# Placing the side work of a layer kernel by estimated engine clocks

## Chip, cores and metric

One core of a Trainium2 chip runs the whole kernel in one launch. The metric is the device time in microseconds, from the first to the last instruction and what lies around it. TensorE is called PE, VectorE DVE, ScalarE ACT, GpSimd POOL and SyncE, which issues nearly all DMAs, SP.

## What is computed

One layer of an encoder over 1280 tokens (1024 of one request, 256 of another), ten tiles of 128 tokens, model width 2048:

```python
hn = rms_norm(x, norm_g)
proj = hn @ w_in                       # 2048 x 4896
xbc, z_ssd, dt_raw, q, k, v, z_att, mq, z_mem = split_cols(proj, IN_SIZES)
xbc = silu(centred_dwconv(xbc, conv_w, conv_b))
y = y_f + y_b + d_skip[:, None] * xs   # chunked state-space scan, forward and backward
o_ssd = rms_norm(y * silu(z_ssd))      # in two groups
o_att = window_attention(q, k, v, sink) * silu(z_att)    # 8 heads, 2 key heads, window 128
o_mem = softmax(mq @ mk.T) @ mv * silu(z_mem)            # 4 heads, 256 memory rows
return x + concat([o_ssd, o_att, o_mem]) @ w_out
# in a chunk of the scan, per head:
decay = exp(where(tril, acs[:, None] - acs[None, :], -inf))
y_diag = ((C @ B.T) * decay) @ (x * dt)
```

## The kernel before

All large products are done in fp32 accuracy with split operands: each operand is a high part in a one-pass format and a low part, and a product is three matmuls (L258, L259, L260; in the paired form L1158, L1159, L1160). ACT makes the high part of a weight row (`wh`, L208), DVE the low part (`wl`, L209). The ten token tiles are two groups of five. The rows of the current group's input stand split in SBUF as `xH` and `xL`, sixteen places of 128 rows each.

Order of the program: memory keys and values; `q` of group 1; paired blocks for the gates and the convolution channels of group 1; `kv` of group 1; `q` of group 0; paired blocks of group 0; then from about 757 us blocks of group 0 (`kv`, `mq`, `z0`, `z1`), of group 1 (`z0`, `z1`, `mq`), and the output projection: four blocks of group 0, and the paired blocks of group 1.

A block (`block_tok`) loops over sixteen weight rows k and five token tiles t, and yields after t = 1, after t = 3 and at the end of a row. At each yield `pump` advances side work, the lanes. A lane is a queue of Python generators; `step` runs one to its next `yield` and so puts its instructions into the program there. Lane 0 holds what attention needs: `mk_prep`, `k_prep`, `attn`, `mem_attn`. Lane 1 holds `dt_prep`, `ssd_one` and `ssd_two`, the scan. Each lane gets a fixed allowance per weight row (`RATES`, some 4 steps), and the number of bare `yield` lines between two parts of a generator sets the time that DMAs and engines have in between. `need` steps a lane until a named piece is done; the refill of the input places with output rows calls it, and a place in the third output block runs all lanes out.

A compile-time scheduler then orders the instructions of each engine; lane instructions of ACT and DVE are held behind the last weight split by `issue_after(marks)`. Each engine works its queue in order, so an instruction that waits holds those behind it.

Pieces that the change touches:
- `attn` loads and normalises the queries of a tile, splits and transposes them (`qh`, `pq`), then for four pairs of heads `scores` (`psc`, two key heads in one step), softmax in the same step, `turn_` (transposes `ppt`, L620), `values` (`po`).
- `mem_attn` the same with memory rows (`pmq`, `pms`, `pmt`, `pmo`).
- `ssd_one` does states and the decay matrix of a tile together. `rows` (L796) loads two broadcast tiles, `rf` and `rb`; `expo` (L866) adds a per-partition bias to each of four column blocks of both; `choose` (L871, L872) merges them and takes one exponential; `weights` (L876) multiplies; `diag` (`py`, L883) is the product.
- `p_fill` (L1189 to L1192) first normalises and splits the input rows of a group. The refill beside group 0's last `z1` block does so again for group 1: load `chd` (L192), scale with `rbc` (L196), split (L199, L200). `x_rows` (`prx`, L1368) makes `rbc`, three times in all.
- Tiles: `wa` five buffers, `wb` four, `rf` two, `rb` three, `ya` two; three PSUM banks `mix` for all lane work.

Of the kernel before, what the change touches and what calls it, by code (L numbers as in the profile page):

```python
# [28 lines left out]
CH, WB, RB, WA, WBB = 4, 3, 4, 5, 4  # L29
RBB = 3  # L30

RATES = {'kv': (2.0, 1.5), 'mq0': (3.9, 4.2), 'z0': (3.9, 4.2), 'z1': (3.9, 4.2), 'mq1': (3.9, 4.2), 'o': (3.5, 3.7)}
# [5 lines left out]
R_G, R_MG, R_SG, R_CB, R_CW, R_N = 0, 16, 32, 40, 52, 112  # L38


@with_exitstack
def hymba_encoder_kernel(
# [7 lines left out]
    V, A, G, T, S = nc.vector, nc.scalar, nc.gpsimd, nc.tensor, nc.sync  # L50
# [21 lines left out]
    dr = ctx.enter_context(tc.tile_pool(name="dr", bufs=1, space=bass.MemoryType.DRAM))  # L72

# [42 lines left out]
    sb_d = [dram([P, 1024], f"sb_{t}") for t in range(NT)]  # L116
    mk_d = dram([P, 4, 256], "mk_d")
# [19 lines left out]
    lanes = (deque(), deque())  # L137
    turn = [0]

    done = set()  # L140
# [7 lines left out]
    def step(lane):  # L148
        name, gen = lane[0]
        try:  # L150

            with ExitStack() as st:
                for ins in marks:
                    st.enter_context(tc.issue_after(ins))
                next(gen)
        except StopIteration:
            lane.popleft()
            done.add(name)

    owed = [0.0, 0.0]  # L160

    def pump(rates):

        for i in range(2):
            owed[i] = owed[i] + rates[i] if lanes[i] else 0.0
        while max(owed) >= 1:
            i = turn[0] ^ 1
            i = turn[0] = i if owed[i] >= 1 else i ^ 1
            owed[i] -= 1
            if lanes[i]:  # L170
                step(lanes[i])

    def need(fn, ts):

        for t in ts:
            while (fn.__name__, t) not in done:
                step(next(x for x in lanes if any(nm == (fn.__name__, t) for nm, _ in x)))


# [56 lines left out]
    def block_tok(w, nt, evac, before_last=None, feats=range(KT), places=range(KT)):  # L236
# [4 lines left out]
        for k in range(KT):  # L241
# [12 lines left out]
            for t in range(nt):  # L254
# [9 lines left out]
                if nt == 5 and t in (1, 3):  # L264
                    yield 0.8 if k == KT - 1 else 0.4
# [91 lines left out]

    def ev_mk(i, ps):
# [9 lines left out]
    def mk_prep(i):  # L368
        kr = w2("mkr")
# [4 lines left out]
        sq = w2("sq")  # L374
        rm = rx[:, 10 + i:11 + i]
        A.activation(sq, kr, AF.Square, scale=rm)
        V.reduce_sum(out=ss, in_=hv(sq, 4), axis=AX.X)
        r = sm.tile([P, 4], F32, tag="s4", name="r", bufs=4)
        rsqrt(r, ss, 1.0 / P, 4)
        yield  # L380
        yield
        V.scalar_tensor_tensor(out=hv(kr, 4), in0=hv(kr, 4), scalar=rm, in1=hb(r, 4, P), op0=ALU.mult, op1=ALU.mult)
        V.tensor_mul(hv(kr, 4), hv(kr, 4), gm.unsqueeze(1).broadcast_to([P, 4, P]))
        yield
        yield
# [4 lines left out]
        if i < 2:  # L390
            A.activation(mkH[:, :, c], hv(ps, 4), AF.Copy)
            V.tensor_sub(mkL[:, :, c], hv(ps, 4), mkH[:, :, c].bitcast(F32))
        else:
            o = w2("mko")
            A.activation(o, ps, AF.Copy)
            S.dma_start(mk_d[:, :, c], hv(o, 4))
        yield

    def mem_values(b):

        S.dma_start(mv, mv_d[:, 2 * b:2 * b + 2, :])
        yield
        yield
# [5 lines left out]
    def mem_swap(_):  # L409

        for b in range(2):
            k = w2("mki")
            S.dma_start(hv(k, 2), mk_d[:, 2 * b:2 * b + 2, :])
            hh = mkH[:, 2 * b:2 * b + 2, :]
# [5 lines left out]
    def k_prep(t):  # L420
        r = w2("kr")[:, :P]
# [3 lines left out]
        yield  # L425
        ss = sm.tile([P, 2], F32, tag="s2", name="kss", bufs=4)
        sq = w2("ksq")[:, :P]
        A.activation(sq, r, AF.Square)
        V.reduce_sum(out=ss, in_=hv(sq, 2), axis=AX.X)
        rr = sm.tile([P, 2], F32, tag="s2", name="krr", bufs=4)  # L430
        rsqrt(rr, ss, 1.0 / 64, 2)
        yield
# [3 lines left out]

        kh = mp.tile([P, 4, 2, 64], F32R, tag="wa", name="kh", bufs=WA)
        for d in range(2):
            A.activation(kh[:, 0:2, d, :], r3, AF.Copy)
        for d in range(2):  # L440
            V.tensor_sub(kh[:, 2:4, d, :], r3, kh[:, 0:2, 0, :].bitcast(F32))
        yield
        yield
        yield
# [8 lines left out]
        yield  # L453

    def kv_shift(_):

        V.tensor_copy(kT[:, :, 0:2 * P], kT[:, :, 3 * P:5 * P].bitcast(F32))
        V.tensor_copy(kL[:, :, 0:2 * P], kL[:, :, 3 * P:5 * P].bitcast(F32))
        V.tensor_copy(v_all[:, 0:2, :], v_all[:, 3:5, :])
        yield  # L460

    def slot(t):
        return t if t < 5 else t - 3

    def dt_prep(t0):
        for t in range(t0, t0 + 5):
            S.dma_start(dt_all[:, t, :], kv_d[t][:, :32])
        yield
        yield
        yield  # L470
# [3 lines left out]
        wj, dd = [a[:, slot(t0):slot(t0) + 5, :].rearrange("p t h -> p (t h)") for a in (wj_all, dd_all)]  # L474
        t5 = lambda a: a.rearrange("p (t h) -> p t h", t=5)
        x = flat(dt_all)
        V.tensor_add(t5(x), t5(x), dtb.unsqueeze(1).broadcast_to([P, 5, 32]))
        e, s = [mp.tile([P, 512], F32, tag="xs", name=n, bufs=2)[:, :160] for n in "es"]
        w, l = [mp.tile([P, 512], F32, tag="ya", name=n, bufs=2)[:, :160] for n in "wl"]
        V.scalar_tensor_tensor(out=e, in0=x, scalar=-1.0, in1=x, op0=ALU.mult, op1=ALU.min)  # L480
        A.activation(e, e, AF.Exp)
        V.tensor_scalar(out=s, in0=e, scalar1=2.0, scalar2=None, op0=ALU.add)
# [3 lines left out]
        V.tensor_scalar(out=e, in0=w, scalar1=1.0 / 17, scalar2=None, op0=ALU.mult)  # L486
        for c in (15, 13, 11, 9, 7, 5, 3):
# [4 lines left out]
        yield  # L492

        da = e
        V.tensor_mul(t5(da), dt_all[:, ts, :], aneg.unsqueeze(1).broadcast_to([P, 5, 32]))
        yield

# [3 lines left out]
        yield  # L501
        yield
        lower = w2("lower")[:, :P]
        G.affine_select(out=lower, in_=ones, compare_op=ALU.is_ge, fill=0.0, base=0,
                        pattern=[[-1, P]], channel_multiplier=1)
        yield
# [5 lines left out]
        ac = wb("ac", shape=(P, 512))  # L512
        A.activation(ac[:, :320], ps[:, :320], AF.Copy)
        for _ in range(2):
            A.activation(s, l, AF.Exp)
            d = da
# [4 lines left out]
            V.scalar_tensor_tensor(out=l, in0=d, scalar=2.0, in1=l, op0=ALU.mult, op1=ALU.add)  # L521
        A.activation(flat(eacs_all), ac[:, 0:160], AF.Exp)
        A.activation(flat(cd_all), ac[:, 160:320], AF.Exp)
        V.tensor_sub(wj, l, ac[:, 0:160])
        V.tensor_add(dd, wj, ac[:, 160:320])
        A.activation(dd, dd, AF.Exp)
        yield
# [3 lines left out]
        acT = wb("acT", shape=(P, 512))  # L531
# [4 lines left out]
        yield  # L536


    def attn(t):
# [8 lines left out]
        q = w2("q")  # L548
        S.dma_start(q, q_d[t])
        yield  # L550
        sq = w2("sq")
        A.activation(sq, q, AF.Square)
        ss = sm.tile([P, 8], F32, tag="s8", name="qss", bufs=4)
        V.reduce_sum(out=ss, in_=hv(sq), axis=AX.X)
        r = sm.tile([P, 8], F32, tag="s8", name="qr", bufs=4)
        rsqrt(r, ss, 1.0 / 64, 8)
        G.tensor_tensor(out=r, in0=r, in1=pow8, op=ALU.mult)
        for _ in range(3):
            yield
        q3 = hv(q)  # L560
        V.tensor_mul(q3, q3, hb(r, 8, 64))
        yield
        qT, parts = [], []
        for b in range(2):
            qh = mp.tile([P, 4, 2, 64], F32R, tag="wa", name="qh", bufs=WA)
            qb = q3[:, 4 * b:4 * b + 4, :]
            A.activation(qh[:, :, 0, :], qb, AF.Copy)
            V.tensor_sub(qh[:, :, 1, :], qb, qh[:, :, 0, :].bitcast(F32))
            parts.append(qh)
            yield  # L570
        yield
        for b, qh in enumerate(parts):
            ps = psum("pq")
            qf = qh.rearrange("p a b d -> p (a b d)")
            for a in range(4):
                T.transpose(ps[:, a * P:(a + 1) * P].bitcast(F32R), qf[:, a * P:(a + 1) * P], identr)
            o = mp.tile([P, 512], F32R, tag="qT", name="qT", bufs=2)
            A.activation(o, ps, AF.Copy)
            qT.append(o)
            yield  # L580
        z = w2("za")
        S.dma_start(hv(z, 4), zT_d[0][grp][:, :, tc_])
        yield
# [3 lines left out]
        def scores(rr):  # L587
            lg = mp.tile([P, 2, 384], F32, tag="lg", name="lg", bufs=2)
            nm = sm.tile([P, 2], F32, tag="m2", name="nm", bufs=10)
            for kv in range(2):  # L590
                h = 4 * kv + rr
                ps = psum("psc")
                st = qT[kv][:, rr * P:(rr + 1) * P]
                T.matmul(ps[:, :nk], st, kT[:, kv, s0 * P:s0 * P + nk], start=True, stop=False)
                T.matmul(ps[:, :nk], st, kL[:, kv, s0 * P:s0 * P + nk], start=False, stop=True)
                V.tensor_tensor_reduce(out=lg[:, kv, :nk], in0=ps[:, :nk], in1=ndist[:, d0:d0 + nk],
                                       scale=-2.0 ** -(h + 1), scalar=nsink[:, h:h + 1], op0=ALU.add, op1=ALU.min,
                                       accum_out=nm[:, kv:kv + 1])
            es = sm.tile([P, 2], F32, tag="m2", name="es", bufs=10)
            G.tensor_tensor(out=es, in0=sk8[:, rr, :], in1=nm, op=ALU.add)  # L600
            den = sm.tile([P, 2], F32, tag="m2", name="den", bufs=10)
# [3 lines left out]
            A.activation(es, es, AF.Exp)  # L605
            V.tensor_add(den, den, es)
            V.reciprocal(out=den, in_=den)
            for kv in range(2):
# [3 lines left out]
        def turn_(rr):  # L612
            lg = state_.pop(rr)
            if rr % 2 == 0:
                state_["pT"] = mp.tile([P, 2, 2, 384], F32, tag="pT", name="pT", bufs=1)
            pT = state_["pT"]
            for kv in range(2):
# [332 lines left out]
    def ssd_two(t):  # L950
# [49 lines left out]
        if first:  # L1000
# [5 lines left out]
            for g in range(2):  # L1006
                turn_ssd(g)
                yield

# [632 lines left out]
```

## Time and profile before

| | |
|---|---|
| median of three runs | 1817.0 us (1814.24 to 1818.96) |
| the profiled execution | 1821.53 us |
| its span, first to last instruction | 1819.8 us |
| mean granted PE clock | 0.994 |
| PE busy | 1777.1 us, 98% |
| ACT, DVE, POOL busy | 1003.1, 1331.6, 676.9 us |
| DMA | 297.49 MB, mean 163 GB/s |

Busy time of PE counts from start to the modelled end of each matmul, and these overlap; a row "A <- B: total, times, longest" in the view of waits is idle time of A's engine that ended when B was done. A row of the view by stretches gives, after start and length, each engine's busy time with the number of its instructions, then granted clock, DMA share and GB/s. A row of a line or tile gives count, then shortest/median/longest in ns, then first and last start in us.

### The profile page before, as it was taken

How to read it: one execution, taken by the hardware profiler on the slowest of the kernel's cores; microseconds unless marked ns; L12 is line 12 of the kernel's file. 1: busy time of each engine (PE TensorE's matmuls, PEld its weight loads, DVE VectorE, ACT ScalarE, POOL GpSimd, SP SyncE). 2: the span in 40 equal slices, each digit the busy share in tenths (PEclk: the TensorE clock that was granted, in tenths of full speed). 3: DMA queues.
4: the chain of work that ended last, by engine and by line, in shares of the span. 5: the costliest groups of instructions: out<-in, count | busy, mean ns of one | idle time of the engine just before them, and what ended most of it. 6: DMA issues, size and time to landing. Idle time of an engine off the chain costs nothing.

```text
span 1819.8 us, 31008 instructions
## 1 busy us (share of the span) xinstructions
PE 1777.1 (98%) x10316; PEld 1573.5 (86%) x10316; DVE 1331.6 (73%) x2447; ACT 1003.1 (55%) x2237; POOL 676.9 (37%) x1092
## 2 busy tenths in 40 slices
PE   9999999999999999999999999999999999999999
PEld 7789999998799999978777778876677788889999
DVE  5595788889768889688768897658875543767665
ACT  6455455445544444456768777767676552433332
POOL 0105888860278889011101110001210010048775
PEclk9999999999999999999999999999999999999999
DMA  8654454446434333485445556657894645644442
GB/s 291 198 175 124 136 145 146 130 147 189 149 114 122 117 100 110 146 233 175 135 135 172 170 171 193 192 166 227 253 279 132 213 147 150 210 135 147 144 141 80
DMA packets 204080, 297.49 MB, mean 163 GB/s; under 512 B 20816, under 2 KB 83600, under 8 KB 203920
## 3 DMA queue, kind: packets, MB, share of 16 engines
q1 hardware_dynamic: 203776, 295.46, 53.0%
q8 instruction: 81, 1.33, 0.3%
q14 instruction: 79, 0.65, 0.1%
q10 hardware_dynamic: 144, 0.06, 0.0%
HBM read 237.18 MB, written 58.26 MB: 162 GB/s over the span
## 4 chain that ended last, share of the span: by engine, by line
PE 70%; DMA 10%; DVE 9%; ACT 4%; POOL 3%; issue 3%; SPq 1%; DVEq 0%; POOLq 0%; ACTq 0%
PE acc L258 9%; PE acc L260 9%; PE acc L259 9%; PE acc L1160 8%; PE acc L1158 8%; PE acc L1159 8%; PE accm L1159 3%; PE accm L1160 3%; PE accm L1158 3%; DVE wl L209 2%; POOL ws L1130 2%; PE ppt L620 1%; DMA wraw<-in_w_in_pairs_dram 1%; PE py L883 1%; PE po L630 1%
## 5 line engine op out<-in xcount | busy, mean ns | idle before, releaser
L258 PE MATMUL acc<-wh,xH 128*128 128x512 f32 (+1 forms) x1248 | 491.9, 394 | 4.4 <-ACT wh L208 3.8
L259 PE MATMUL acc<-wl,xH 128*128 128x512 f32 (+1 forms) x1248 | 477.7, 383 | 2.1 <-DVE wl L209 2.1
L260 PE MATMUL acc<-wh,xL 128*128 128x512 f32 (+1 forms) x1248 | 478.6, 384 | 0.0
L209 DVE TENSOR_TENSOR wl<-wraw,wh 128x512 fp32r<-128x512 f32 (+1 forms) x480 | 353.9, 741 | 132.3 <-ACT wh L208 127.8
L208 ACT ACTIVATE wh<-wraw 128x512 fp32r<-128x512 f32 (+1 forms) x480 | 290.5, 612 | 184.7 <-PE acc L260 124.1
L1130 POOL TENSOR_TENSOR ws<-wraw 128x128 f32<-128x128 f32 x224 | 143.5, 641 | 365.6 <-DMA wraw<-in_w_in_pairs_dram 199.3
L258 PEld LDWEIGHTS acc<-wh,xH 128*128 128x128 f32 x1248 | 236.0, 189 | 48.7 <-issue 6.8
L259 PEld LDWEIGHTS acc<-wl,xH 128*128 128x128 f32 x1248 | 236.4, 189 | 44.3 <-issue 4.3
L260 PEld LDWEIGHTS acc<-wh,xL 128*128 128x128 f32 x1248 | 235.9, 189 | 44.6 <-issue 2.8
L208 ACT ACTIVATE sh<-ws 128x384 fp32r<-128x384 f32 x224 | 116.0, 523 | 277.1 <-POOL ws L1130 141.0
L209 DVE TENSOR_TENSOR sl<-ws,sh 128x384 fp32r<-128x384 f32 x224 | 158.5, 710 | 135.3 <-ACT sh L208 127.2
L1130 POOL TENSOR_TENSOR ws<-wraw,ws 128x128 f32<-128x128 f32 x224 | 151.4, 676 | 17.3
L1130 POOL TENSOR_TENSOR ws<-ws,wraw 128x128 f32<-128x128 f32 x224 | 153.8, 687 | 0.0
L1130 POOL TENSOR_TENSOR wraw<-wraw 128x128 f32<-128x128 f32 x224 | 135.5, 605 | 17.3
L1160 PE MATMUL acc<-xH,wl 128*128 128x320 f32 x320 | 99.8, 312 | 2.1 <-DVE wl L209 1.6
L1159 PE MATMUL acc<-tL,sh 128*128 128x320 f32 x320 | 98.9, 309 | 0.0
L1160 PE MATMUL accm<-tH,wl 128*128 128x320 f32 x320 | 98.9, 309 | 0.0
L1158 PE MATMUL acc<-xH,wh 128*128 128x320 f32 x320 | 98.8, 309 | 0.0
L1159 PE MATMUL accm<-tL,wh 128*128 128x320 f32 x320 | 98.8, 309 | 0.0
L1158 PE MATMUL accm<-tH,wh 128*128 128x320 f32 x320 | 98.7, 308 | 0.0
L1158 PE MATMUL acc<-tH,sh 128*128 128x320 f32 x320 | 98.6, 308 | 0.0
L1160 PE MATMUL acc<-tH,sl 128*128 128x320 f32 x320 | 98.1, 307 | 0.0
(483 smaller groups left out, 3929.1 us busy)
## 6 DMA issues: line engine op xcount, KB each, us to landing
wraw<-in_w_in_pairs_dram SPq DMA_DIRECT2D x160, 256.0 KB, 2.7
wraw<-in_w_in_laid_dram SPq DMA_DIRECT2D x128, 256.0 KB, 3.2
wraw<-in_w_out_laid_dram SPq DMA_DIRECT2D x64, 256.0 KB, 2.9
wraw<-in_w_out_pairs_dram SPq DMA_DIRECT2D x64, 256.0 KB, 2.9
rf<-ac SPq DMA_DIRECT2D x40, 256.0 KB, 4.0
rb<-ac SPq DMA_DIRECT2D x40, 256.0 KB, 4.5
wraw<-in_w_mem_laid_dram SPq DMA_DIRECT2D x32, 256.0 KB, 4.6
ra<-in_x_turned_dram SPq DMA_DIRECT2D x16, 320.0 KB, 3.2
```

Of the source, the lines that this page charges most:

```text
L208: a = A.activation(h, raw, AF.Copy)
L209: b = V.tensor_sub(l, raw, h.bitcast(F32))
L258: T.matmul(ps[t][:, :n], sh, h[:, :n], start=(k_ == 0), stop=False)
L259: T.matmul(ps[t][:, :n], sh, l[:, :n], start=False, stop=False)
L260: T.matmul(ps[t][:, :n], sl, h[:, :n], start=False, stop=(k_ == KT - 1))
L620: T.transpose(pt[:, a * P:(a + 1) * P], lg[:, kv, a * P:(a + 1) * P], ident)
L630: T.matmul(hv(po[kv * 64:kv * 64 + 64, :2 * P], 2), v_all[:, s0 + a, kv * 64:kv * 64 + 64], pT[:, kv, :, a * P:(a + 1) * P], start=(a == 0 ...
L883: T.matmul(py[:, h * 64:h * 64 + 64], mt[:, (h % 4) * P:(h % 4 + 1) * P], xsT[g][:, h * 64:h * 64 + 64], start=True, stop=True)
L1130: G.tensor_tensor(out=o, in0=x, in1=y, op=op)
L1158: T.matmul(ps[p], h, xh, start=(k_ == 0), stop=False)
L1159: T.matmul(ps[p], h, xl, start=False, stop=False)
L1160: T.matmul(ps[p], l, xh, start=False, stop=(k_ == 7))
```

## The change

It replaces the fixed allowances by a small model that runs while the program is written. `Clocks` keeps an estimated time per engine, and for each tile when it will be full and when free, from a cost per instruction. Every generator now yields what its next step wants (tiles, PSUM banks, other pieces), and `pump` steps a lane only if that is estimated ready. There are four lanes: attention, scan, preparation, decay. Allowances double, `block_tok` yields after every tile, and scores and transposes of attention are one step per key head. Query preparation moves out of `attn` and `mem_attn` (`q_prep`, `m_prep`), and the decay matrix out of `ssd_one` (`decay`). Group 1's split rows are stored in `p_fill` and loaded by the refill. In `expo` and `decays`, the bias of `rf` is the difference of both, the merge comes next, and the second bias rides on the exponential. `wa` gets three buffers and a new `wm` two.

```diff
-CH, WB, RB, WA, WBB = 4, 3, 4, 5, 4
+CH, WB, RB, WA, WM, WBB = 4, 3, 4, 3, 2, 4
-RATES = {'kv': (2.0, 1.5), 'mq0': (3.9, 4.2), ..., 'o': (3.5, 3.7)}
+RATES = {'kv': (4, 4), 'mq0': (8, 8), ..., 'o': (8, 8)}
+DEBT = 6.0
+AHEAD, QUEUE = 300.0, 4000.0
+    def ran(self, e, ins, power=False):
...
+        at = self.now[e] if e != "SP" else self.now["PE"]
+        for x in srcs:
+            at = max(at, self.full.get(self.name(x), 0.0))
+        for x in outs:
+            at = max(at, self.free.get(self.name(x), 0.0))
+        if e == "SP":
+            end = at + 2600 + self.size(outs[0]) * 1.5
+        else:
+            end = self.now[e] = at + cost + 20
...
+    def ready(self, want):
+        tiles, n = want[:2]
+        at = [self.full.get(self.name(x), 0.0) - (0 if n else AHEAD) for x in tiles]
+        at += [self.opens("mix", 3, i + 1) - 400 * i for i in range(n)]
+        at += [self.now[e] - QUEUE for e in ("ACT", "DVE")]
+        return max(at) <= self.now["PE"]
...
     def pump(rates):
-        for i in range(2):
-            owed[i] = owed[i] + rates[i] if lanes[i] else 0.0
-        while max(owed) >= 1:
-            i = turn[0] ^ 1
-            i = turn[0] = i if owed[i] >= 1 else i ^ 1
+        for i in range(4):
+            owed[i] = min(owed[i] + rates[i % 2], DEBT) if lanes[i] else 0.0
+        while True:
+            i = next((j for j in (ATT, PREP, SSD, DEC) if may(j)), None)
+            if i is None:
+                return
             owed[i] -= 1
...
-                if nt == 5 and t in (1, 3):
-                    yield 0.8 if k == KT - 1 else 0.4
+                if nt == 5 and t < 4:
+                    yield 0.4 if k == KT - 1 else 0.2
...
         def expo(q):
-            for d, r in enumerate(rows_[q]):
-                for j in range(4):
-                    c = slice(j * P, (j + 1) * P)
-                    h = 16 * d + 4 * q + j
-                    A.activation(r[:, c], r[:, c], AF.Identity, bias=wj_all[:, slot(t), h:h + 1])
+            r = rows_[q][0]
+            for j in range(4):
+                c = slice(j * P, (j + 1) * P)
+                A.activation(r[:, c], r[:, c], AF.Identity, bias=wj_all[:, t, 4 * q + j:4 * q + j + 1])
         def choose(q):
             V.copy_predicated(hv(mt, 4), upper...., hv(rf, 4))
-            A.activation(mt, mt, AF.Exp)
+        def decays(q):
+            r = rows_[q][1]
+            for j in range(4):
+                c = slice(j * P, (j + 1) * P)
+                h = 16 + 4 * q + j
+                A.activation(r[:, c], r[:, c], AF.Exp, bias=wj_all[:, t, h:h + 1])
...
+            if grp == 1:
+                for d, y in zip(row_d[k + 8 * i], (h, l)):
+                    S.dma_start(d, y.bitcast(F32))
...
+    def fill_stored(k):
+        for d, y in zip(row_d[k], new_place(k)):
+            S.dma_start(y.bitcast(F32), d)
+        yield
+        yield
...
-        scores(0)
-        yield
-        scores(1)
-        yield
-        yield
-        turn_(0)
...
+        order = "A0 A1 B0 C0 B1 D0 C1 E0 A2 D1 B2 E1 A3 C2 B3 D2 V0 C3 E2 D3 E3 V1"
+        for what, rr in [(x[0], int(x[1])) for x in order.split()]:
+            if what == "A":
+                for kv in range(2):
+                    yield wants(qT[kv], banks=1)
+                    scores(rr, kv)
...
+            elif what == "E":
+                for kv in range(2):
+                    yield wants(state_[rr], banks=1)
+                    turn_(rr, kv)
```

More of the change, by code (lines that the diff above doesn't have):

```diff
@@ L41, in hymba_encoder_kernel, with wants @@
+def wants(*tiles, banks=0, after=()):
+    return tiles, banks, after
 @with_exitstack
@@ L134, in hb @@
         return ap.unsqueeze(2).broadcast_to([P, n, d])
-    lanes = (deque(), deque())
+    lanes = [deque() for _ in range(4)]
+    ATT, SSD, PREP, DEC = range(4)
+    wanted = [None] * 4
     turn = [0]
-    done = set()
+    said = set()
     def queue(lane, fn, ts):
@@ L146, in hymba_encoder_kernel, with step @@
     marks = []
-    def step(lane):
-        name, gen = lane[0]
+    def step(i):
+        name, gen = lanes[i][0]
+        clk.lane = True
         try:
@@ new lines, in m_prep @@
+    def m_prep(t):
+        q = w2("mq")
+        S.dma_start(q, mq_d[t])
+        yield wants(q)
+        sq = w2("sq")
+        A.activation(sq, q, AF.Square)
+        yield wants(sq)
+        ss = sm.tile([P, 4], F32, tag="s4", name="mss", bufs=4)
+        V.reduce_sum(out=ss, in_=hv(sq, 4), axis=AX.X)
+        r = sm.tile([P, 4], F32, tag="s4", name="mr", bufs=4)
+        rsqrt(r, ss, 1.0 / P, 4)
+        yield wants(q, banks=1, after=scored("mem_attn", t))
+        ps = psum("pmq")
+        for h in range(4):
+            turned(ps[:, h * P:(h + 1) * P], q[:, h * P:(h + 1) * P])
+        qh = mp.tile([P, 512], F32R, tag="qT", name="mqh", bufs=2)
+        A.activation(qh, ps, AF.Copy)
+        yield wants(qh)
+        ql = mp.tile([P, 512], F32R, tag="qT", name="mql", bufs=2)
+        V.tensor_sub(ql, ps, qh.bitcast(F32))
+        turned_q["mem_attn", t] = qh, ql, r
@@ L471, in dt_prep @@
+    def dt_prep(t0):
+        t5 = lambda a: a.rearrange("p (t h) -> p t h", t=5)
+        work, more = [mp.tile([P, 2, 384], F32, tag="lg", name=n, bufs=2).rearrange("p a c -> p (a c)")
+                      for n in ("dtw", "dtm")]
+        e, s, w, l = [work[:, 160 * i:160 * i + 160] for i in range(4)]
+        x, lower = more[:, 448:608], more[:, 320:448]
+        for t in range(5):
+            S.dma_start(t5(x)[:, t, :], kv_d[t0 + t][:, :32])
+        yield wants(x)
         grp = t0 // 5
@@ L561, in attn @@
[L561 to L580, printed above, removed]
@@ L763, in ssd_one @@
             xc.append(x)
-        for _ in range(6 if t == NS - 1 else 8 if t == 4 else 3):
-            yield
+        yield wants(bc, banks=1, after=prior(t, "weighed"))
         ps = psum("pcb")
@@ L776, in ssd_one @@
         A.activation(cb, hv(ps[:, :256], 2), AF.Copy)
-        yield
+        cb_of[t] = cb
+        said.add(("ssd_one", t, "cb"))
+        xsT = []
+        for g in range(2):
+            yield wants(xc[g], banks=1, after=prior(t) + (("dt_prep", t // 5 * 5),))
+            ps = psum("pxs")
+            for j in range(4):
+                turned(ps[:, j * P:(j + 1) * P], xc[g][:, j, :])
+            xt = mp.tile([P, 512], F32, tag="xs", name="xs", bufs=2)
+            V.tensor_copy(xt, ps)
+            xsT.append(xt)
+        xs_of[t] = xsT
+        yield wants(cb)
         cd2 = wb("cd2", shape=(P, 2, P))
@@ L790, in rows, with decay @@
+    def decay(t):
+        first = t in (NS - 1, NT - 1)
+        yield wants(after=(("dt_prep", t // 5 * 5),) + ((("ssd_two", NS - 1),) if t == NT - 1 else ()))
+        mts, rows_ = {}, {}
         def rows(q):
@@ L953, in ssd_two @@
         tok = slice(t * P, (t + 1) * P)
+        yield wants(after=(("decay", t // NS * NS),))
         ss = sm.tile([P, 2], F32, tag="s2", name="yss", bufs=4)
@@ L979, in ssd_two @@
             y, z, st = ld[g]
+            yield wants(y, z, *(() if last else (cc, state)), banks=0 if last else 1)
             if not last:
@@ L1562, in hymba_encoder_kernel @@
             if j0 + k == -7:
-                for x in lanes:
-                    while x:
-                        step(x)
+                for i in range(4):
+                    while lanes[i]:
+                        force(i)
                 beside.close()
```

728 lines of the change are left out of this document (421 added, 307 removed).

## The prediction

> **What bounds the kernel now.** I read the page's first block, then busy time by stage, then who makes TensorE (PE) wait, then the granted clock around the long waits.
>
> ```profile
> span 1819.8 us, 31008 instructions
> PE 1777.1 (98%) x10316; PEld 1573.5 (86%) x10316; DVE 1331.6 (73%) x2447; ACT 1003.1 (55%) x2237; POOL 676.9 (37%) x1092
> ```
> ```profile
> 0.00:757.00 757.00, 747.18 (x4623) 707.91 (x4624) 588.63 (x939) 377.05 (x710) 434.58 (x682) 1.00 0.49 148
> 757.00:1500.00 743.00, 715.35 (x3840) 572.66 (x3839) 545.98 (x1198) 507.26 (x1319) 90.61 (x154) 0.99 0.61 188
> 1500.00:1622.00 122.00, 120.53 (x538) 99.38 (x537) 72.04 (x118) 47.83 (x80) 13.23 (x20) 1.00 0.53 161
> 1622.00:1819.80 197.80, 194.08 (x1321) 193.56 (x1320) 124.97 (x194) 71.02 (x129) 138.49 (x236) 1.00 0.44 133
> ```
>
> The columns after the length are PE, its weight loads, VectorE (DVE), ScalarE (ACT), GpSimd, then clock, DMA share and GB/s. PE is the bound in every stage. The lanes, which this change rewrites, run from 757 to 1500 us. PE stands idle there for 743.00 - 715.35 = 27.7 us, against 9.8 before and 1.5 + 3.7 behind. No PE work of a lane goes away but one row of statistics, so what can be won in this stage is waiting. Who causes it:
>
> ```profile
> PE ppt L620 <- ACT lg L609: 4.1, 4, 2.0
> PE pmq L124 <- DMA mq<-mq: 3.6, 1, 3.6
> PE py L883 <- DVE rb L876: 3.0, 4, 1.7
> PE pxs L124 <- DVE nm L596: 2.8, 1, 2.8
> PE pmk L388 <- DMA wraw<-in_w_in_laid_dram: 2.0, 1, 2.0
> PE psc L594 <- ACT qT L578: 1.7, 1, 1.7
> ```
>
> Every waiter in this list is a lane's own matmul (a transpose, a score, a state product) that PE reached before its operand; none is a matmul of the projections. A lane matmul that is early stops the projections queued behind it. Some of these waits cost a second time:
>
> ```profile
> 816.00:819.90 3.90, 2.19 (x18) 2.00 (x17) 3.79 (x8) 0.79 (x4) 0.00 (x0) 1.00 0.59 195
> 819.90:823.30 3.40, 3.40 (x9) 2.64 (x9) 2.53 (x7) 1.01 (x3) 2.06 (x2) 0.50 0.61 200
> 946.20:953.00 6.80, 6.39 (x23) 5.20 (x24) 4.98 (x16) 4.66 (x15) 0.19 (x1) 0.50 0.48 179
> 953.00:959.80 6.80, 6.80 (x35) 5.22 (x33) 5.67 (x18) 6.18 (x16) 0.87 (x2) 1.00 0.15 35
> 1434.30:1441.10 6.80, 5.91 (x20) 5.07 (x21) 1.38 (x2) 3.14 (x7) 1.20 (x2) 0.50 0.92 295
> ```
>
> After a wait the clock is granted at 0.50 for 3.4 or 6.8 us, and PE starts 23 matmuls in 6.8 us where the next 6.8 us hold 35. The three stretches hold 3.40 + 6.39 + 5.91 = 15.7 us of busy time; half of it, 7.9 us, is lost. Waiting and its echo are worth 27.7 + 7.9 = 35.6 us, about 2% of the span: the ceiling of what placing the steps better can bring by these rows.
>
> The Trainium skill, page "TensorE: Matmul & The Clock Gate", section "Part 1: The HAM clock gate (the "warmup" mystery)", says that the clock halves after an idle window of about 3.4 us and that the granted share is only ever a half or whole. The second agrees. The first does not: of the 3.9 us ahead of 819.9, PE was busy in 2.19, and the clock fell all the same. By the page only the one wait of 3.6 us would be followed by a slow stretch, and the echo would be 5.91 / 2 = 3.0 us instead of 7.9. The rows decide, and I use 7.9.
>
> **The change, part by part.**
>
> *Steps placed by estimated clocks, in four lanes.* Before, a lane advances by a fixed allowance for each row of weights, and a yield stands for "surely ready by now". Afterwards a step with PE work goes in when its operands and a PSUM bank are estimated ready, and no step while ACT or DVE is estimated over 4 us ahead. Of the 27.7 us of idle PE I take two thirds as gone, -18.4. Bounds: 0, since the estimate may miss as the fixed yields do, and -27.7. I stay below the upper end because two of the six rows above wait on a DMA, whose estimate here is 2.6 us plus 1.5 ns an element (3.4 us for 512), and the transfers it must foresee land later than that:
>
> ```profile
> DMA to landing us min/median/max: 3.1/4.3/6.7
> ```
>
> That is the broadcast load of the decay rows (L796) in this stage. Of the clock's echo the same two thirds, -5.2 (0 to -7.9). Late next are these loads, then the DVE results.
>
> Part of a wait hides under the modelled ends of matmuls and shows only on the weight loads, which also show what one more break in PE's stream costs:
>
> ```profile
> PEld ppt L620 <- ACT lg L609: 8.8, 16, 2.4
> PEld acc L258 <- issue: 6.8, 24, 0.4
> PEld acc L259 <- issue: 4.3, 18, 0.2
> ```
>
> The transposes' loads waited 8.8 us where PE shows 4.1; of that 4.7 I take 3 as won (0 to -4.7).
>
> *Finer steps.* Scores and transposes of attention go out one key head at a time: 16 PE steps a tile instead of 8, so 80 more over ten tiles, at five places a row of weights instead of three. The first weight load of the projections behind a burst waits (6.8 + 4.3) / 42 = 0.26 us in the rows above. All 80 apart would cost +21; ready neighbours go out in one burst and then it is 0. I take a quarter, +5, since one pass of the pump issues every neighbour that is ready.
>
> *Input rows come back from DRAM.* While the rows of token group 1 are first split (78 to 134 us), both halves are also stored, 32 stores of 320 KB; the refill beside group 0's last block then issues 32 loads in place of 16 loads and 48 ACT and DVE operations. A third of the row statistics (`x_rows`) goes too.
>
> ```profile
> L199 ACT ACTIVATE xH<-chd x24: 723/730/757, 955.0 to 1285.5; 128x640 fp32r<-128x640 f32 x24
> L200 DVE TENSOR_TENSOR xL<-chd,xH x24: 802/818/826, 961.7 to 1292.2; 128x640 fp32r<-128x640 f32 x24
> L192 SPq DMA_DIRECT2D chd<-in_x_turned_dram x16: 327/333/577, 738.2 to 1069.9; - x16
> L196 DVE SCALAR_TENSOR_TENSOR chd<-chd,vec,rbc x16: 862/877/892, 817.9 to 1084.3; 128x640 f32<-128x640 f32 x16
> 75.69 1.11 PE prx L1368 x10
> ```
>
> DVE is relieved of 16 x (0.877 + 0.818) = 27.1 us and ACT of 16 x 0.730 = 11.7. Both lie beside PE, so nothing directly. The statistics are on PE: 10 matmuls, 1.1 us in the chain of waits, -1.1 (its copies on DVE are beside). The stores:
>
> ```profile
> 78.00:134.00 56.00, 56.00 (x248) 46.36 (x247) 55.63 (x92) 32.69 (x51) 0.00 (x0) 1.00 0.58 175
> ACT wh L208 <- PE acc L260: 5.2, 5, 1.5
> 1034.00:1130.00 96.00, 94.87 (x514) 76.11 (x514) 81.52 (x170) 68.83 (x176) 11.06 (x15) 1.00 0.60 188
> zT<-th SPq DMA_DIRECT2D x16, 320.0 KB, 2.6
> ```
>
> 10.5 MB in 56 us is 187 GB/s on top of 175. At 175 for a share of 0.58, that asks for 1.2 of what the queues carry, so the stores run some 10 us longer than the stage; the weight loads are queued among them. What hides it: the split of the weights (`wh`) in that window waits for PE to free its buffer, never for a DMA, so the weights are there early. I cost it at 0; uncovered, a store's 2.6 us would come up once for each of eight fills, +21. On SyncE's queue a store waits for the DVE half, and weight loads stand behind it; the same cover holds. The refill adds 5.2 MB to a stage at 0.60, and its loads wait for PE to be done with the old rows, with weight loads behind them on SyncE. 48 more DMA issues at 0.33 us are 16 us of a queue that is not on the path: 0.
>
> *One bias pass.*
>
> ```profile
> L866 ACT ACTIVATE rf<-rf,wj_all x160: 384/388/438, 791.9 to 1427.0; 128x128 f32<-128x128 f32 x160
> L866 ACT ACTIVATE rb<-rb,wj_all x160: 384/388/434, 793.9 to 1438.9; 128x128 f32<-128x128 f32 x160
> L872 ACT ACTIVATE rb<-rb x40: 612/630/636, 802.6 to 1442.6; 128x512 f32<-128x512 f32 x40
> ```
>
> The 160 biases on `rb` go, and 40 exponentials of 512 columns become 160 of 128 with a bias. The trace has no such exponential; the nearest row is the biased pass of the same shape, 388 ns (bounds: 0.630 / 4 = 158 ns and 434). At 388, ACT saves 40 x 0.630 = 25.2 us. ACT was busy 507 of 743 us, so 0 on the path; it shortens `rb`'s chain to the wait on L876 above, which is in the first term.
>
> *Buffers.* The work tiles go from five shared to three plus two, and the preparation of queries gets a lane of its own that holds up to three: 0 here, a rival below.
>
> Sum: -18.4 - 5.2 - 3.0 + 5.0 - 1.1 = -22.7 us. The profiled execution took 1821.5 us (span 1819.8) and becomes 1798.8; the median of the runs, 1817.0, is 4.5 below it, so I forecast 1794.
>
> **The rivals.**
>
> *Waiting all but gone.* Every term at its far end with bursts merged: -27.7 - 7.9 - 4.7 - 1.1 = -41, 1776. For it: all waits named are of the kind that the estimate sees. Against: the DMA landings above.
>
> *The waits move.* The bank, the three work tiles and late loads hold PE as long as the yields did, the breaks eat the rest: -3, 1814. For it: PE is busy 96% of the stage already, and each wait is small.
>
> *The preparation lane starves (slower).*
>
> ```profile
> L664 SPq DMA_DIRECT2D mq<-mq x10: 422/426/1390, 1078.6 to 1475.9; - x10
> DMA mq<-mq: 18.7, 8
> 1500.00:1540.00 40.00, 40.00 (x179) 33.10 (x178) 12.32 (x20) 9.04 (x15) 0.00 (x0) 1.00 0.49 147
> ```
>
> With three tiles the next query load can't go out until the one before is turned. If the lane falls behind, the refill of the output rows and the closing of the lanes force its steps unready, and PE meets the load's landing: 2.3 us each (18.7 / 8), up to the 3.6 seen. There are 20 such loads. It decides from 22.7 / 3.6, some seven exposed at full clock; with half clock behind half of them (3.4 us lost each), twelve give 43 + 20 - 23 = +40, nine about +25, 1842. Against it: 40 us and more of pure projections (1500 to 1540) stand behind the last lane work, ahead of the place where lanes are closed, and an advance of up to eight steps a row replaces some four.
>
> **How the numbers follow.** Forecast, gain of 8 to 35 us: 0.50. Almost gone, more than 35: 0.16. Waits move, from 5 slower to 8 faster: 0.19. Starved: 0.15. A difference under 0.3% (5.5 us) can't be told from none here; of the third case 0.04 gains more than that. So faster 0.70, same 0.15, slower 0.15. The likeliest case alone spans 1782 to 1809. To leave out no more than 2 in 10 the range reaches to 1770 (below the first rival's 1776) and 1822, which leaves out the starved case with its 0.15 and some 0.05 below.
>
> **What would show it.** Right: idle PE from 757 us to the end of lane work falls from 27.7 to about 10; no or one stretch at clock 0.50 in it; no wait of a lane's matmul above 1.5 us; the first 757 us as long as now within 2 us; `xL<-chd` down to 8 operations; L866's pass 160 instead of 320. Wrong: idle time that stays near 28 with waits on DMAs or PSUM evacuations; projections that wait for `wl`; a clump of lane matmuls just ahead of the refill or the close; more weight-load waits put down to issue than 50; weight splits that wait for a DMA between 78 and 134 us.

## The result, and the profile after

The changed kernel takes 1792.3 us (median of four runs, 1788.5 to 1795.7) against 1816.5 for the kernel before: a ratio of 0.9866, 95% interval 0.9842 to 0.9890. That is 24 us less; on the chip of the first experiments it was 20 us less (1810.7 to 1790.5). The two profiled executions differ by more, 1821.5 against 1788.5, since the one before lies above its median and the one after below.

The first block of its page, and busy time in the four stages that were shown of before:

```profile
span 1786.8 us, 30971 instructions
PE 1762.2 (99%) x10306; PEld 1574.1 (88%) x10306; DVE 1302.3 (73%) x2417; ACT 974.9 (55%) x2181; POOL 668.4 (37%) x1092
```
```profile
0.00:761.00 761.00, 749.79 (x4616) 709.48 (x4617) 587.96 (x937) 378.50 (x709) 435.28 (x682) 1.00 0.52 160
761.00:1466.00 705.00, 696.63 (x3830) 570.54 (x3830) 518.29 (x1169) 477.11 (x1264) 81.19 (x154) 1.00 0.66 206
1466.00:1588.00 122.00, 121.11 (x538) 99.68 (x536) 70.44 (x117) 47.57 (x79) 12.04 (x19) 1.00 0.54 161
1588.00:1786.80 198.80, 194.63 (x1326) 194.37 (x1326) 125.65 (x196) 71.74 (x129) 139.91 (x239) 1.00 0.43 133
```

The lane stage went from 743 to 705 us, the stage ahead of it from 757 to 761; the rest is as it was. In the lane stage PE is idle for 8.4 us instead of 27.7 and the clock is never halved. It starts 3830 matmuls instead of 3840, the ten of the row statistics. Who still makes PE wait there (in the changed kernel all instructions carry the line of one helper, L128, so tiles tell them apart):

```profile
PE ppt L128 <- DVE nm L128: 1.4, 1, 1.4
PE pxs L128 <- DMA xc<-xbc_d: 1.0, 1, 1.0
PE pms L128 <- DVE moT L128: 1.0, 1, 1.0
PE py L128 <- ACT mpT L128: 0.9, 1, 0.9
PE pms L128 <- DVE mql L128: 0.9, 1, 0.9
PE po L128 <- ACT pT L128: 0.8, 1, 0.8
```

Single waits of about 1 us are left, no wait reaches 1.5 us, and only one of these is for a DMA.

The page does not show a second effect: how often PE changes between projections and lane work. I counted the places where a lane matmul follows a projection in the order of start, from the last `kv` evacuation to the end of the third output block. There are 293 bursts before and 208 after. From the start of a projection matmul to that of the first lane matmul behind it takes 0.344 us on average before and 0.265 after. The fall is in the long steps. The median step is 0.234 us before and 0.231 after, and from one projection to the next it is 0.228 and 0.227, so a break without a wait costs a few ns. But 89 steps took over 0.3 us before and 25 after, and what these took beyond 0.228 us fell from 32.8 to 7.2 us in all. PE busy time between the same marks:

```profile
775.90:1563.00 787.10, 761.49 (x3995) 608.43 (x3994) 562.05 (x1218) 518.39 (x1335) 86.79 (x148) 0.99 0.60 185
```
```profile
781.10:1530.60 749.50, 741.89 (x3983) 606.36 (x3984) 533.13 (x1186) 488.88 (x1280) 77.58 (x148) 1.00 0.65 202
```

The first row is of the kernel before, the second of the changed one. This stage is 37.6 us shorter: 18.0 of idle PE, about 7.9 of half clock, 1.1 of statistics, and 10.6 more of busy PE. The 25.6 us that the long steps lost account for most of the 18.0 and 10.6 together, so I read the 10.6 as short waits hidden under the modelled ends of matmuls.

Ahead of the lanes 4 to 5 us are lost (5.2 in this profile, of which one more stretch at half clock, 3.4 us long, is 1.7). The stage of the stores, and who waited around it in the changed kernel (PE, then ACT, then the queue of SP from 78 to 160 us, then two weight loads on its timeline):

```profile
78.00:134.00 56.00, 54.53 (x240) 44.60 (x239) 50.58 (x83) 30.79 (x49) 0.00 (x0) 1.00 0.88 302
```
```profile
PE acc L128 <- ACT qs L128: 1.9, 1, 1.9
PE acc L128 <- ACT wh L128: 1.5, 1, 1.5
```
```profile
ACT wh L128 <- DMA wraw<-in_w_in_laid_dram: 5.1, 3, 3.2
```
```profile
SPq L128 <- ACT xH L128: 17.0, 13, 2.2
SPq L128 <- DVE wl L128: 9.8, 5, 6.6
SPq L128 <- DVE xL L128: 6.4, 13, 0.9
```
```profile
92.16 0.43 SPq L128 DMA_DIRECT2D wraw<-in_w_in_laid_dram  x1
106.96 0.96 SPq L128 DMA_DIRECT2D wraw<-in_w_in_laid_dram  x1
```

SP stands 23 us for stores whose data is not split yet. Between 92 and 107 us it issues no weight load, the split waits for a weight, and PE for the split. The clock is then halved once, and the same again near 491 us behind another wait:

```profile
154.00:156.50 2.50, 0.65 (x5) 0.39 (x3) 0.00 (x0) 1.35 (x4) 0.94 (x3) 1.00 0.61 231
156.50:159.90 3.40, 3.27 (x11) 2.87 (x12) 1.30 (x2) 2.59 (x7) 0.00 (x0) 0.50 0.81 275
```

### The profile page after: what moved, and what is told of

It reads as the page before. It is cut to its first block, busy times and chain, and to the rows that moved or that the text cites. A ratio compares the mean times of both kernels' runs of the same rounds, so it can differ in the third digit from the quotient of the medians.

```text
span 1786.8 us, 30971 instructions
## 1 busy us (share of the span) xinstructions
PE 1762.2 (99%) x10306; PEld 1574.1 (88%) x10306; DVE 1302.3 (73%) x2417; ACT 974.9 (55%) x2181; POOL 668.4 (37%) x1092
## 4 chain that ended last, share of the span: by engine, by line
PE 81%; issue 6%; DMA 5%; DVE 4%; ACT 2%; POOL 1%; SPq 0%; DVEq 0%; ACTq 0%; POOLq 0%
PE acc L128 58%; PE accm L128 11%; PE py L128 2%; PE psc L128 1%; PE po L128 1%; DVE wl L128 1%; PE pst L128 1%; PE ppt L128 1%; DMA rf<-ac 1%; PE pmo L128 1%; PE pms L128 1%; PE pyf L128 1%; PE pyb L128 1%; DMA wraw<-in_w_in_pairs_dram 1%; DMA rb<-ac 0%
## 5 line engine op out<-in xcount | busy, mean ns | idle before, releaser
L128 PE MATMUL acc<-wh,xH 128*128 128x512 f32 (+1 forms) x1248 | 490.7, 394 | 4.2 <-ACT wh L128 3.7
L128 DVE TENSOR_TENSOR wl<-wraw,wh 128x512 fp32r<-128x512 f32 (+1 forms) x480 | 353.1, 740 | 173.9 <-ACT wh L128 169.8
L128 PE MATMUL acc<-wl,xH 128*128 128x512 f32 (+1 forms) x1248 | 475.1, 381 | 2.8 <-DVE wl L128 2.6
L128 PE MATMUL acc<-wh,xL 128*128 128x512 f32 (+1 forms) x1248 | 472.6, 379 | 0.0
L128 ACT ACTIVATE wh<-wraw 128x512 fp32r<-128x512 f32 (+1 forms) x480 | 291.7, 614 | 200.4 <-PE acc L128 125.7
L128 POOL TENSOR_TENSOR ws<-wraw 128x128 f32<-128x128 f32 x224 | 144.7, 646 | 400.4 <-DMA wraw<-in_w_in_pairs_dram 202.9
L128 PEld LDWEIGHTS acc<-wh,xH 128*128 128x128 f32 x1248 | 234.9, 188 | 51.1 <-issue 7.0
L128 PEld LDWEIGHTS acc<-wl,xH 128*128 128x128 f32 x1248 | 235.2, 188 | 48.7 <-issue 6.5
L128 PEld LDWEIGHTS acc<-wh,xL 128*128 128x128 f32 x1248 | 234.6, 188 | 44.5 <-issue 1.0
L128 ACT ACTIVATE sh<-ws 128x384 fp32r<-128x384 f32 x224 | 116.3, 524 | 275.6 <-POOL ws L128 132.3
L128 DVE TENSOR_TENSOR sl<-ws,sh 128x384 fp32r<-128x384 f32 x224 | 157.1, 704 | 136.8 <-ACT sh L128 134.8
L128 POOL TENSOR_TENSOR ws<-wraw,ws 128x128 f32<-128x128 f32 x224 | 153.4, 685 | 17.3
L128 POOL TENSOR_TENSOR ws<-ws,wraw 128x128 f32<-128x128 f32 x224 | 152.8, 682 | 0.0
L128 POOL TENSOR_TENSOR wraw<-wraw 128x128 f32<-128x128 f32 x224 | 134.9, 602 | 17.3
L128 PE MATMUL acc<-xH,wl 128*128 128x320 f32 x320 | 100.1, 313 | 1.7 <-DVE wl L128 1.4
L128 PE MATMUL acc<-tH,sh 128*128 128x320 f32 x320 | 99.1, 310 | 1.9 <-ACT qs L128 1.9
L128 PE MATMUL acc<-tH,sl 128*128 128x320 f32 x320 | 99.2, 310 | 0.0
L128 PE MATMUL acc<-xL,wh 128*128 128x320 f32 x320 | 98.9, 309 | 0.0
L128 PE MATMUL accm<-tH,wl 128*128 128x320 f32 x320 | 98.8, 309 | 0.0
L128 PE MATMUL acc<-xH,wh 128*128 128x320 f32 x320 | 98.7, 309 | 0.0
L128 PE MATMUL accm<-tL,wh 128*128 128x320 f32 x320 | 98.7, 308 | 0.0
L128 PE MATMUL accm<-tH,wh 128*128 128x320 f32 x320 | 98.7, 308 | 0.0
```

The costliest lines, as they stand in the source:

```text
L128: r = f(*a, **kw)
```

## The experiments

Theory A: the placing of the steps by estimated readiness gives the gain. Theory B: a good part is relief, 27 us of DVE work and 25 to 37 us of ACT work less in the stage. The ratio is to the kernel before, run on the same chip. The runs e1 to e4 shared one chip (before: 1810.7 us), e5 to e8 a second (1811.4) and e9 to e12 a third (1814.7), so a difference between runs of different chips is surer by the ratios than by the medians.

| run | median us | ratio, 95% interval |
|---|---|---|
| e1_again | 1790.5 | 0.9886 (0.9872 to 0.9899) |
| e2_old_refill | 1795.0 | 0.9908 (0.9895 to 0.9922) |
| e3_late_store | 1791.8 | 0.9886 (0.9871 to 0.9900) |
| e4_two_bias | 1801.3 | 0.9941 (0.9927 to 0.9955) |
| e5_no_gate | 1889.9 | 1.0431 (1.0417 to 1.0444) |
| e6_head_pairs | 1799.6 | 0.9939 (0.9926 to 0.9952) |
| e7_old_placing | 1822.6 | 1.0057 (1.0044 to 1.0070) |
| e8_pool_store | 1784.1 | 0.9850 (0.9837 to 0.9863) |
| e9_ahead | 1801.4 | 0.9915 (0.9892 to 0.9938) |
| e10_act_copy | 1787.8 | 0.9845 (0.9815 to 0.9875) |
| e11_pool_dma | 1805.6 | 0.9945 (0.9927 to 0.9963) |
| e12_placing_only | 1806.3 | 0.9943 (0.9921 to 0.9964) |

**The changed kernel again.**

> The changed kernel as it is, as the measure for the other runs on the same chip. Both theories: 1792 us within 3, a stage of lanes (761 to 1466 us) with 8 to 10 us of idle PE, and some 11 us of idle PE before it.

1790.5 us. The other runs are read against it.

**The estimate switched off.**

```diff
-        return max(at) <= self.now["PE"]
+        return True
```

> The changed kernel with the estimate switched off: a lane's step goes in as soon as its allowance lets it, only the order between pieces is kept. Theory A (the estimate of readiness gives the gain): lane matmuls come ahead of their operands, idle PE in the lane stage goes from 8 back to 25 us or more with stretches at half clock, 1808 us or more. Theory B (relief of the engines, and a softmax cut into steps, give it): idle PE stays under 15 us and the time under 1798.

1889.9 us. Between the marks used above, of this run:

```profile
789.20:1633.80 844.60, 783.29 (x3987) 620.07 (x3986) 534.27 (x1180) 490.77 (x1279) 77.38 (x147) 0.97 0.57 178
```
```profile
PE pacs L128 <- DVE dtw L128: 8.8, 1, 8.8
PE acc L128 <- DVE wl L128: 8.0, 5, 5.2
PE ppt L128 <- ACT lg L128: 6.2, 6, 1.6
```

PE is idle for 61.3 us, 58 us run at half clock, and now even the projections wait for their weights' low part (`wl`), which stands behind lane work on DVE. Four lanes, finer steps and doubled allowances without the estimate are far worse than two lanes with fixed yields. The estimate is needed; this does not yet say that all 24 us are its own.

**The other two edits under the old placing.** The kernel before, with the stores, `fill_stored` and the one bias pass:

> The kernel before, with its two lanes and fixed yields, and with the other two edits: rows stored and loaded back, one bias pass. Theory A: the stores cost some 4 us ahead of the lanes, and relief brings nothing on the path: 1809 to 1817, no faster than the kernel before by more than 2 us. Theory B: the relief shows here too, 8 us or more: below 1803.

1822.6 us, 11 more than the kernel before. Of its profile:

```profile
781.50:1559.50 778.00, 755.30 (x3985) 601.36 (x3984) 537.81 (x1186) 490.15 (x1278) 79.05 (x148) 1.00 0.62 194
```

The lane stage starts 5.6 us later, as in the changed kernel. It is 778.0 us long, just what the 787.1 of before give less their half clock and the statistics. 24 us less of DVE work and 28 less of ACT work brought nothing on the path. Theory B falls in this form. The rest of the 11 us is not settled: this profile is the fastest of its runs. Part of it is half clock, since the granted clock falls as the runs get longer (0.998 at 1817.8 us, 0.992 at 1825.8).

**Undoing one edit under the new placing.**

```diff
-            r = rows_[q][0]
-            for j in range(4): ... AF.Identity, bias=wj_all[:, t, 4 * q + j:4 * q + j + 1]
+            for d, r in enumerate(rows_[q]):
+                for j in range(4): ... AF.Identity, bias=wj_all[:, t, 16 * d + 4 * q + j:...]
...
-            for j in range(4): ... AF.Exp, bias=wj_all[:, t, h:h + 1]
+            A.activation(r, r, AF.Exp)
```

> The changed kernel with the old two bias passes and one exponential over 512 columns. Theory A: ScalarE gets 25 us of work back in a stage where it is busy 477 of 705 us, nothing on the path: 1792 us within 4. Theory B: 1798 us or more, with PE waiting for the decay tiles.

> The changed kernel with the old refill of group 1's rows: nothing is stored, the rows are loaded from the input, scaled and split again, and the third row statistics are back. Theory A (the placing of the steps gives the gain): the first 757 us get back some 4 us that the stores cost, the lane stage stays within 5 us of the changed kernel's 705: 1787 to 1793 us. Theory B (relief of VectorE and ScalarE gives a good part of the gain): 27 us of VectorE work come back into the stage and it grows by 8 us or more: 1797 us or more.

Two bias passes: 1801.3 us, +10.7 on e1. The old refill: 1795.0, +4.4 net, with the lane stage starting 5.2 us earlier (776.1 against 781.3 us) but 10 longer. The two bias passes went as theory B has it, against e7, and so did the old refill's stage; its time lies between the two theories. So either the work counts under the new placing, or both edits only led to another order of the steps. Two runs tell these apart.

```diff
-AHEAD, QUEUE = 300.0, 4000.0
+AHEAD, QUEUE = 200.0, 4000.0
```

> The changed kernel with one constant moved: a step without PE work may go in 200 ns ahead of its operands in place of 300. It adds and removes no work, and shows how far the time hangs on the exact order of the steps. If orders of this kind are worth little: 1790 within 3. If the 5 to 11 us that the old refill and the two bias passes cost under the new placing are mostly another order: this one differs by as much, 1795 us or more.

1801.4 us, +10.8 on e1, with not one instruction of work more. By the ratios to the kernel before it is 0.3%, some 5 us, and the intervals overlap; but e10 below, which ran on the same chip as e9 and nearly keeps the changed kernel's order, is 13.6 us faster. The stage between the marks is 758.8 us, 9.3 longer than in the changed kernel's profile:

```profile
785.50:1544.30 758.80, 745.71 (x3983) 604.92 (x3984) 534.07 (x1186) 488.46 (x1280) 83.20 (x148) 1.00 0.65 199
```

And the reverse, ACT work without another order:

```diff
             A.activation(r[:, c], r[:, c], AF.Exp, bias=wj_all[:, t, h:h + 1])
+        A.engine.activation(r, r, AF.Copy)      # 512 columns, not seen by the estimate
```

> The changed kernel with 40 more ScalarE copies of 512 columns (0.62 us each, 25 us in all), in place on the finished decay tile and unknown to the estimate, so that the lane steps stand where they stood. If ScalarE's work and its place in the decay chain make what the two bias passes cost: 1797 to 1803. If it is what the placing makes of a longer estimate: 1790 within 3.

1787.8 us: no loss. ACT's busy time between the marks went up to 510.2 us and the stage stayed 750.3:

```profile
778.20:1528.50 750.30, 743.25 (x3987) 607.79 (x3986) 535.16 (x1190) 510.15 (x1321) 76.01 (x148) 1.00 0.65 202
```

The added copies, in that kernel's instructions by tile (shortest, median and longest time in ns, first and last start in us):

```profile
L1088 ACT ACTIVATE rb<-rb x40: 614/624/638, 816.7 to 1374.4; 128x512 f32<-128x512 f32 x40
```

The two bias passes have nearly the same amount of ACT work and a longer stage:

```profile
779.80:1543.70 763.90, 747.21 (x3987) 608.85 (x3986) 535.95 (x1187) 508.09 (x1321) 80.66 (x148) 1.00 0.64 198
```

So the amount of ACT's work is not what they cost. The traces show what differs: put PE's matmuls in the order of their starts, and projections and lane pieces alternate in e1 exactly as in the changed kernel and in e10 but for one place, while in e9 and in the two bias passes another order begins within the first 60 us of the lane stage. That leaves the order to which the longer estimate leads as the likely cause. The two bias passes also wait for both broadcast loads before the first of them, and no run has that by itself. For the old refill the order is likely too, but there DVE work was not added by itself, so it stays an argument.

**The placing by itself.** Both other edits undone:

> The changed kernel with both other edits undone, the old refill and two bias passes: the placing alone. If the three parts add up (1790, +4 and +11): 1805, 6 us under the kernel before. If the placing carries the gain by itself and the rest was a matter of order: 1797 or less. If it needs the relief: 1811, no gain.

1806.3 us, a ratio of 0.9943: 8 us under the kernel before on its chip. By the medians the sum of the parts held; by the ratios the other two edits are worth 10 us together, not 15. The lane stage is 771.0 us:

```profile
777.90:1548.90 771.00, 751.43 (x3990) 607.58 (x3989) 558.64 (x1216) 518.76 (x1337) 85.50 (x148) 0.99 0.61 189
```

The longest kind of wait of PE left there, in the waits of that kernel:

```profile
PE pyb L128 <- DMA cc<-xbc_d: 3.9, 2, 3.0
```

Between e12 and the changed kernel the placing is the same rule. All kernels with it but the ungated have 205 to 216 bursts and stages of 749 to 771 us, against 280 and 293 bursts and 778 and 787 us with the fixed yields. The ungated one has 236 bursts, so part of their fall comes with the four lanes and the new pump and not with the estimate. So the placing by itself, with its lanes, buffers and finer steps, is worth about 10 us here. Another 10 to 15 us hang largely on the order that these constants give with this very list of instructions; moving one constant by 100 ns makes the stage 8 to 9 us longer.

**Finer steps.** Scores and transposes of both key heads in one step, wanting two banks:

```diff
-                for kv in range(2):
-                    yield wants(qT[kv], banks=1)
-                    scores(rr, kv)
+                yield wants(*qT, banks=2)
+                for kv in range(2):
+                    scores(rr, kv)
```

> The changed kernel with scores and transposes of attention again in one step for both key heads, which then wants two PSUM banks. If finer steps cost breaks in PE's stream, as the prediction has it: about 5 us less, 1785. If the pump puts ready neighbours out together anyway: 1790 within 3, with about the 208 bursts of lane work that the changed kernel has (the kernel before has 293), or some us more from waiting for two banks.

1799.6 us, 9 slower, with the same 208 bursts and 16.0 us of idle PE:

```profile
PE psc L128 <- ACT pT L128: 2.2, 2, 1.5
PE po L128 <- ACT pT L128: 1.7, 2, 1.1
```

Finer steps cost no breaks: the pump puts ready neighbours out together. The order of PE's work is another one here too. Whether the 9 us are the second bank or that order, this run can't say.

**The stores.** Moved to the paired blocks, one behind a weight load each, and then left where they were but issued by POOL:

```diff
                 for d, y in zip(row_d[k + 8 * i], (h, l)):
-                    S.dma_start(d, y.bitcast(F32))
+                    G.dma_start(d, y.bitcast(F32))
```

> The changed kernel with the 32 stores moved from the split of the rows into the paired blocks of group 1, one behind a weight load each. If the stores' DMA load between 78 and 134 us makes the waits at 112 and 156 us, these go and the time falls by 3 to 5 us: about 1788. If the waits are of another cause, 1792, and the waits stay. Theories A and B say the same here.

> The changed kernel with the 32 row stores issued by GpSimd, which is idle from 78 to 134 us, in place of SyncE. If the early waits come from weight loads that stand behind stores on SyncE's queue: the first 776 us get their 5 us back, 1786. If they come from the transfers' own load on the DMA engines (share 0.88 there): 1790, and PE still waits for weights between 105 and 160 us.

Late stores: 1791.8 us, no gain. The first `q` block came back to 154.3 us from 159.4, but the paired blocks took 288.8 us instead of 283.5. One stretch at half clock more, 3.4 us, is 1.7 of that; the rest is not explained, since SP's queue does not wait for the stores' data there. POOL's queue: 1784.1 us, the fastest with its interval clear of e1's, 6 us under it:

```profile
78.00:134.00 56.00, 56.00 (x249) 46.34 (x248) 52.53 (x88) 30.71 (x48) 15.46 (x28) 1.00 0.90 315
```

The stores of the high rows by tile, and then what SP's queue waits for most from 78 to 160 us, in the same kernel:

```profile
L128 POOL DMA_DIRECT2D rowH<-xH x16: 542/542/793, 80.4 to 137.7; - x16
```
```profile
SPq L128 <- DVE wl L128: 40.4, 19, 8.5
```

The DMA engines are as loaded as before (0.90, 315 GB/s), yet PE is busy for all of the 56 us, and the stores' waits are gone from SP's queue, which now waits above all for weight buffers to come free. PE takes its matmuls in the same order as in the changed kernel. So in that stage it was the order on SP's queue, not the load on the DMA engines. The lanes start 2.8 us earlier than in e1 (778.5 us) and their stage is 2 us shorter; the two profiled executions differ by 5.1 us, the medians by 6.4.

**A later estimate for DMAs**, on top of the POOL stores (3600 in place of 2600):

> The changed kernel with the row stores on GpSimd's queue and an estimated landing of DMAs 1 us later (3.6 us plus 1.5 ns an element). If late DMAs still make PE wait (some 2 us of waits for chunk loads): 1780 to 1784. If the later estimate holds the lanes back, so that lane work piles up at the refill and in the output blocks: 1786 or more.

1805.6 us, 21 slower than e8. The stage is 769.0 us, with 19.7 us of idle PE; the waits are now for ACT and DVE (`psc` behind `cb` 3.7 us, behind `moT` 3.4), and three output blocks instead of two run long. A better guess of one duration made the whole worse.

## Why the prediction was right, and where not

The time was forecast at 1794 and is 1792.3. The path was right: lane matmuls that PE reached too early went. That the number came so close is partly luck. In the two profiled executions the terms come to -18.0 - 7.9 - 10.6 - 1.1 + 5 = -32.6 us, where the sum had -22.7. The medians moved by 24, largely since the profiled run of before lost more to half clock than its usual runs do. Terms were wrong in both directions.

- *Idle PE, -18.4.* Between the marks 25.6 became 7.6, -18.0. The kind of wait named was the one that went. Two thirds was met by this order of steps: the same rule leaves 13.1 us in e9, 16.0 in e6 and 19.6 in e12. What e5 shows is that the new lanes need the estimate (61.3 us idle without it), not that all 18 are its own.
- *Its echo in the clock, -5.2.* In the two profiles all of the 17.1 us at half clock went, some -7.9. A usual run has less of it to lose. The mean granted clock was 0.994 in the profiled run of before, but 0.996 to 0.998 on average in its runs on the three chips of the experiments, and 0.998 in those of the changed kernel. From these, an estimate: 4 to 7 us lost to half clock before and 4 after, so the term was 0 to -3 for the medians.
- *Hidden waits, -3, and finer steps, +5.* Together +2, and measured -10.6. The step that failed is "80 more breaks" at 0.26 us each. Bursts fell from 293 to 208. By the pump's loop, a lane that waits until it is ready has several steps ready at once, and they go out in one place; e6, with as many bursts, shows that finer steps add none. And the price was wrong: 0.26 us was the mean of the 42 weight loads that waited, beside 293 bursts, and it is not time of PE. A break without a wait costs PE a few ns on the way in (0.234 against 0.228 us), and the first projection behind a burst starts 0.084 us after the last lane matmul in both kernels (median). The hidden waits were sized too small: I took them from the transposes alone, at most 4.7. The sign that I named, more than 50 weight loads that wait for issue, did come (57, 14.4 us) and said nothing of the bursts.

```profile
PEld acc L128 <- issue: 14.4, 57, 0.4
```

- *The stores, 0.* They cost 5 us in the profile. The mechanism was in the text, weight loads behind a waiting store on SP, and so was the price if uncovered. Failed has the cover: the row that I took for it, a split that waits for PE and never for a DMA, was of a queue without the stores in it. The sign named for this came: two splits waited 3.6 us together for a DMA between 78 and 134 us. A lead of the weights is used up when no load goes out for 15 us.
- *Relief, 0.* Held by e7 for both engines under the old placing, and by e10 for ACT under the new one. The exponential with a bias takes 392 ns, the 388 of the nearest row.
- *Statistics, -1.1.* Ten matmuls are gone.
- *The rivals.* The starved lane did not come: the waits left are not for query loads, and no lane work piles up at the close. "Waiting all but gone" is near what the lane stage shows in the profile (-37.6), less the 5 us of the stores.
- *The clock rule.* Here too the clock fell behind a wait of 1.9 us (156.5 us) with PE at work in 0.65 of the 2.5 us ahead; the page of the Trainium skill named in the prediction ("TensorE: Matmul & The Clock Gate", Part 1) has it fall after an idle window of about 3.4 us. The rows stand.

## What to carry to other kernels

When side work shares an in-order engine with the main stream, place a step when its operands are expected, not after a fixed number of turns; many of the waits go (the placing alone won 8 us here). Take the time of such a kernel as one draw: run it with a constant moved a little before you credit an edit with 10 us. A store that waits for its data does not belong in the queue that feeds the weights, and moving the stores behind later weight loads on that queue won nothing; an idle engine's queue gave the version that beats both, 1784.1 us.

## What was not expected

One constant of the placing, 100 ns out of 300, was worth some 9 us of the lane stage, nearly as much as undoing an edit with 25 us of ACT work; adding that ACT work without moving a step cost nothing. The DMA engines carried 315 GB/s at a share of 0.90 without one PE wait in those 56 us. A DMA issued from POOL took 542 ns of its time, one from SP 326.
